# A hybrid attention and expert block: the first norm's factors applied behind the transposes of the first two tiles

## Chip, cores, metric

One core of a Trainium2 chip runs the whole block in one launch. The metric is the device time in microseconds. A profile names the engines PE (TensorE), DVE (VectorE), ACT (ScalarE), POOL (GpSimd) and SP (SyncE, which issues most DMAs).

## The reference

One layer on x of 1024 tokens by 1024 columns in float32, then a final norm:

```
hn   = rms_norm(h, norm_mix_g)
proj = hn @ w_in
y_dil, y_na = dilated_mixture_attention(...), neighbourhood_attention(...)
h = h + concat(rms_norm(y_dil), rms_norm(y_na)) @ w_out
h = h + hierarchical_moe(rms_norm(h, norm_ffn_g), ...)
return rms_norm(h, norm_final_g)
```

`rms_norm(x, gain)` scales each token (row) by `rsqrt(mean(x * x) + 1e-6)` and each column by its gain. The gain `norm_mix_g` holds 1024 factors, one per column of x. Here the change touches only how the first `rms_norm` reaches the product with `w_in`.

## The kernel before

Tokens are worked on in eight tiles of 128. The order of the work is written out by hand: the code's order is the order in each engine's queue, and a framework adds the semaphore waits. Matrix products keep float32 accuracy by splitting each operand into a high part and a rest (`split`, L102 to L104: ScalarE writes `hi` as a rounded copy, the subtraction of `hi` from the source gives `lo`, on VectorE or, with `pool=True`, on GpSimd); a product is three matmuls, hi·hi, hi·lo and lo·hi.

The stage that the change touches is the first one (L173 to L320). It norms x, transposes it so that the model's columns lie on the partitions (`xhi`, `xlo`, kept for all projections), and computes the values `v` of both attentions. Its parts:

- `x_stages(T)` (L192), a generator that is run step by step: Square with the row's sum on ScalarE, then mean and eps, Sqrt on ScalarE, the reciprocal, the scaling of x by the row's number and by `g_b` (L207, two halves of 512 columns). `g_b` holds the 1024 factors, repeated on all 128 partitions by one DMA (`bcast_row`, L126). After these four steps come two halves that each transpose four blocks of 128x128 into one PSUM bank (`ps_s`, `ps_pt`, L212) and split the bank into `xhi` and `xlo`.
- `wv_load` and `wv_split` (L182, L186) load and split a quarter of the value weights, two blocks of 128 rows each; `v_chunk(ps, T, w, c)` (L218) is the six matmuls of tile T with quarter c; `v_out` and `v_store` split and store the finished tile.
- Ahead of the data, TensorE runs 13 dummy matmuls on zeros (L242). ScalarE's first instruction is a Sqrt of a tile `one` (L255) that VectorE fills (L254), so that its table is loaded early.

SP issues in this order: x of tile 0, the identity, `g_b`, two quarters of the weights, x of tile 1, the other two quarters, x of tiles 2 and 3. TensorE's order is: dummies, tile 0's transposes, tile 0 with quarters 0 and 1, tile 1's transposes, tile 1 with quarters 0 and 1, tile 0 with quarters 2 and 3, tile 2's transposes, tile 1 with quarters 2 and 3, then tile by tile. The second projection of values, eight head pairs of attention, the output product and sixteen experts follow; the line L401 with L402 that the prediction speaks of is the split of a query bank in two pieces of 64 partitions each in the attention stage.

Of the kernel before, what the change touches and what calls it, by code (L numbers as in the profile page):

```python
# [9 lines left out]
F32 = mybir.dt.float32  # L10
F32R = mybir.dt.float32r
BF = mybir.dt.bfloat16
I32 = mybir.dt.int32
AF = mybir.ActivationFunctionType
ALU = mybir.AluOpType
# [57 lines left out]
def build(nc, tc, a, ctx, dbg=None):  # L73
    dbg = dbg or {}
    f = lambda t: t.bitcast(F32)
# [21 lines left out]
    ident = const.tile([128, 128], F32, name="ident")  # L97

    def bank(tag):
        return psum.tile([128, 512], F32, name="ps_" + tag, tag=tag)  # L100

    def split(hi, lo, src, pool=False):  # L102
        nc.scalar.activation(hi, src, AF.Copy)  # L103
        (nc.gpsimd if pool else nc.vector).tensor_tensor(lo, src, f(hi), op=ALU.subtract)  # L104
# [17 lines left out]
    def run(gen, n=1):  # L122
        for _ in range(n):
            next(gen, None)

    def bcast_row(dst, src, n):  # L126
        nc.sync.dma_start(dst, bass.AP(tensor=src.tensor, offset=src.offset, ap=[[0, 128], [1, n]]))
# [17 lines left out]
    with ExitStack() as att:  # L145
        xhi = [xt_pool.tile([128, 8, 512], F32R, name="xhi%d" % z, tag="xhi%d" % z) for z in range(2)]
        xlo = [xt_pool.tile([128, 8, 512], F32R, name="xlo%d" % z, tag="xlo%d" % z) for z in range(2)]
# [20 lines left out]
        def zero_low():  # L168
            for pair in k_low:
                for h, t in enumerate(pair):  # L170
                    nc.gpsimd.memset(f(t)[64 - 64 * h:128 - 64 * h, :], 0.0)

        with ExitStack() as ph:  # L173
            xp = ph.enter_context(tc.tile_pool(name="xp", bufs=2))
            wv = ph.enter_context(tc.tile_pool(name="wv", bufs=1))
            xs, raws = {}, {}
# [5 lines left out]
            def wv_load(c0, c):  # L182
                raws[c] = f(qk.tile([128, 1024], F32R, name="k_hh", bufs=4)).rearrange("p (k c) -> p k c", k=2)
                nc.sync.dma_start(raws[c], w_in.rearrange("(k p) c -> p k c", p=128)[:, 2 * c:2 * c + 2, c0:c0 + 512])

            def wv_split(c, pool=False):  # L186
                hi = wv.tile([128, 2, 512], F32R, name="wv_hi%d" % c)
                lo = wv.tile([128, 2, 512], F32R, name="wv_lo%d" % c)
                split(hi, lo, raws.pop(c), pool)
                return hi, lo  # L190

            def x_stages(T):  # L192

                xt = xs.pop(T)
                xn = xp.tile([128, 1024], F32, name="xn")
                ss = xp.tile([128, 1], F32, name="ss")
                nc.scalar.activation(xn, xt, AF.Square, accum_out=ss)
                yield
                nc.vector.tensor_scalar(ss, ss, 1.0 / 1024, EPS, op0=ALU.mult, op1=ALU.add)
                yield  # L200
                nc.scalar.activation(ss, ss, AF.Sqrt)
                yield
                r = xp.tile([128, 1], F32, name="rstd")
                nc.vector.reciprocal(r, ss)
                for q in range(2):
                    c = slice(512 * q, 512 * q + 512)
                    nc.vector.scalar_tensor_tensor(xn[:, c], xt[:, c], r, g_b[:, c], op0=ALU.mult, op1=ALU.mult)  # L207
                yield
                for q in range(2):
                    pt = bank("pt" if q else "s")  # L210
                    for k in range(4):
                        nc.tensor.transpose(pt[:, k * 128:(k + 1) * 128],  # L212
                                            xn[:, (4 * q + k) * 128:(4 * q + k + 1) * 128], ident)
                    s = slice(None), slice(4 * q, 4 * q + 4), slice(T % 4 * 128, (T % 4 + 1) * 128)
                    split(xhi[T // 4][s], xlo[T // 4][s], pt.rearrange("p (k t) -> p k t", k=4))
                    yield

            def v_chunk(ps, T, w, c):  # L218
                for k in range(2 * c, 2 * c + 2):
                    t = slice(T % 4 * 128, (T % 4 + 1) * 128)  # L220
                    for n, (x, l) in enumerate(((xhi, 0), (xhi, 1), (xlo, 0))):
                        nc.tensor.matmul(ps, x[T // 4][:, k, t], w[c][l][:, k % 2, :],
                                         start=k == 0 and n == 0, stop=k == 7 and n == 2)
# [15 lines left out]
            idle = xp.tile([128, 512], BF, name="idle", bufs=1)  # L239
            nc.gpsimd.memset(idle, 0.0)  # L240
            ps = bank("o")
            for _ in range(13):  # L242
                nc.tensor.matmul(ps, idle[:, 0:128], idle, start=True, stop=True)
            zero_low()
            nc.sync.dma_start(ident, a["ident"])
            g_b = wv.tile([128, 1024], F32, name="g_b")
            bcast_row(g_b, a["norm_mix_g"], 1024)
            wv_load(1024, 0)
            wv_load(1024, 1)
            x_load(1)  # L250
            for c in range(2, 4):
                wv_load(1024, c)
            one = xp.tile([128, 1], F32, name="one", bufs=1)
            nc.vector.memset(one, 1.0)  # L254
            nc.scalar.activation(one, one, AF.Sqrt)  # L255
            xt = {T: x_stages(T) for T in range(8)}
            run(xt[0], 4)
            w = {0: wv_split(0)}
            run(xt[0], 2)
            w[1] = wv_split(1)  # L260
            pv = [bank("mm"), bank("o")]
            v_chunk(pv[0], 0, w, 0)
            run(xt[1], 4)
            for c in range(2, 4):
                w[c] = wv_split(c, True)
# [17 lines left out]
            for T in range(2, 8):  # L283
                ps = bank("mm" if T % 2 else "o")
# [19 lines left out]
            for T in range(8):  # L304
                ps = bank("mm" if T % 2 else "o")
# [114 lines left out]
        ap = att.enter_context(tc.tile_pool(name="att", bufs=2))  # L420
# [279 lines left out]
        who, wlo, raws, yd, yt, hx = {}, {}, {}, {}, {}, {}  # L700
# [99 lines left out]
        for k in range(1, 8):  # L800
            s0 = 16 * (k - 1)
# [10 lines left out]
        for k in range(8):  # L812
            s = 104 + 2 * k if k < 4 else 106 + 2 * k
# [38 lines left out]
        ps, pts = {}, {}  # L852
        for s in range(len(steps) + 4):
            at = s % 16
            before = pairs[s // 16 - 1] if s >= 16 else None
            if s < len(steps):
                p, h, n = steps[s]
# [7 lines left out]
            if s - 2 in ps:  # L865
                q, g, m = steps[s - 2]
# [6 lines left out]
            if s - 3 in pts:  # L873
                q, g, m = steps[s - 3]
# [6 lines left out]
            if s + 6 < len(steps):  # L881
                if n == 2 and s > 8:
                    p.late_loads(h)
                after, g, _ = steps[8 * (s // 8) + 8] if s < 120 else (None, 0, 0)
# [264 lines left out]
    with ExitStack() as ph:  # L1149
# [113 lines left out]
        for T in range(8):  # L1263
            yn = y_norm(T)
            ns = norm_stages(T - 1) if T else None
            for c in range(2):
                ps = bank("mm")
# [93 lines left out]
    def new_x(name="xg"):  # L1361
        return ex.tile([128, 1024], F32, name=name, bufs=2)
# [367 lines left out]
    with tc.If(n_top > 256), tc.tile_pool(name="fb", bufs=1) as fb:  # L1730
# [10 lines left out]
        with tc.For_i(0, 16, 1) as e:  # L1741
# [9 lines left out]
            for q in range(6):  # L1751
                with tc.If(n_e > 256 + 128 * q):
                    x = new_x("xg1")
# [3 lines left out]
        for e in (14, 15):  # L1757
            W = whole(split_up([load_up(e, z) for z in range(2)], 0)) + split_down(load_down(e))
            n_e, = counts(ORDER[e], ORDER[e] + 1, mybir.ALL_ENGINES)
            for q in range(2):  # L1760
                with tc.If(n_e > 128 * q):
                    x = new_x("xg1")
# [32 lines left out]
```

## Time and profile before

| | |
|---|---|
| times of three runs | 888.94, 889.92, 892.41 us; median 889.92 |
| the profiled execution | 892.44 us, of which the span is 890.7 us |
| mean granted clock of TensorE over the span | 0.976 |
| busy: TensorE, VectorE, ScalarE, GpSimd | 832.3, 558.5, 510.0, 220.9 us |

The span is what the profiler sees of the engines; the device time has a little more around it. Times of single instructions below count from the start of the span. [...]

### The profile page before, as it was taken

What the parts mean: (1) busy time and instruction counts of PE and PEld (TensorE: products, weight loads), DVE (VectorE), ACT (ScalarE), POOL (GpSimd) and SP (SyncE); (2) the same over time, 40 slices, a digit from 0 to 9 for tenths busy, and PEclk for the clock granted to TensorE, in tenths of its full rate; (3) what the DMA queues carried; (4) which work ended last, traced back from release to release, by engine and by line L of the source; (5) the groups of instructions that cost most, each with busy time, mean ns of one, the idle gap of its engine ahead of it and who ended that gap; (6) DMA issues with size and microseconds to landing.
All of it is one profiled execution on the core that took longest, in us unless ns stands there. A gap on an engine that the chain in (4) does not pass through costs nothing. (4 is left out here: it accounts for less than half of the span.)

```text
span 890.7 us, 13312 instructions
## 1 busy us (share of the span) xinstructions
PE 832.3 (93%) x4492; PEld 693.2 (78%) x4492; DVE 558.5 (63%) x1249; ACT 510.0 (57%) x1079; POOL 220.9 (25%) x180
## 2 busy tenths in 40 slices
PE   8999999989999999999898999999799999999880
PEld 5888878979889888878787887887577787777760
DVE  4551125776767767666677753677786566959573
ACT  5441127757667576677575633543585566858570
POOL 4001122221232302332411100000442344635403
PEclk8999999999999999999999999998999999999995
DMA  6855452314343141534346747995798987999663
GB/s 238 286 210 165 126 159 65 105 48 108 96 136 105 54 137 48 148 100 120 76 160 195 265 144 239 357 343 216 233 354 250 317 220 209 357 324 304 181 257 121
DMA packets 129919, 168.72 MB, mean 189 GB/s; under 512 B 14875, under 2 KB 101403, under 8 KB 129824
## 3 DMA queue, kind: packets, MB, share of 16 engines
q1 hardware_dynamic: 119904, 143.58, 49.8%
q0 software_dynamic: 9936, 24.16, 9.8%
q8 instruction: 41, 0.67, 0.3%
q14 instruction: 38, 0.31, 0.1%
HBM read 129.93 MB, written 47.47 MB: 199 GB/s over the span
## 5 line engine op out<-in xcount | busy, mean ns | idle before, releaser
L103 ACT ACTIVATE pt_hi<-ps_pt 128x512 fp32r<-128x512 f32 (+2 forms) x128 | 67.6, 528 | 70.8 <-PE ps_pt L509 41.7
L378 PE MATMUL ps_mm<-xhi,w_lo 128*128 128x512 f32 x256 | 105.1, 411 | 1.1 <-POOL w_lo L104 1.1
L378 PE MATMUL ps_mm<-xlo,w_hi 128*128 128x512 f32 x256 | 105.0, 410 | 0.0
L378 PE MATMUL ps_mm<-xhi,w_hi 128*128 128x512 f32 x256 | 102.9, 402 | 0.0
L104 DVE TENSOR_TENSOR pt_lo<-ps_pt,pt_hi 128x512 fp32r<-128x512 f32 (+2 forms) x128 | 77.2, 603 | 31.8 <-ACT pt_hi L103 31.1
L104 POOL TENSOR_TENSOR w_lo<-w_raw,w_hi 128x1024 fp32r<-128x1024 f32 x16 | 38.3, 2392 | 229.5 <-ACT w_hi L103 229.5
L424 DVE CUSTOM_DVE_ANT_0 p<-ps_s,bias 128x256 f32<-128x256 f32 (+1 forms) x192 | 81.8, 450 | 18.2 <-PE ps_s L411 10.8
L104 DVE TENSOR_TENSOR g_lo<-raw_up,g_hi 128x1024 fp32r<-128x1024 f32 x64 | 75.5, 1220 | 25.2 <-ACT g_hi L103 25.1
L1419 PE MATMUL ps_mm<-g_hi,x_hi 128*128 128x512 f32 x184 | 76.0, 413 | 0.5 <-ACT x_hi L103 0.5
L1419 PE MATMUL ps_mm<-g_hi,x_lo 128*128 128x512 f32 x184 | 74.2, 403 | 2.2 <-DVE x_lo L104 2.2
L1419 PE MATMUL ps_mm<-g_lo,x_hi 128*128 128x512 f32 x184 | 73.9, 402 | 0.0
L430 ACT ACTIVATE p<-p,stats 128x256 f32<-128x256 f32 x128 | 63.7, 500 | 9.6 <-DVE stats L424 9.1
L103 ACT ACTIVATE g_hi<-raw_up 128x1024 fp32r<-128x1024 f32 x64 | 64.4, 1067 | 1.8 <-DMA raw_up<-in_w_up 0.8
L411 PE MATMUL ps_s<-k_hh,q_s 128*128 128x256 f32 (+1 forms) x192 | 60.7, 324 | 4.0 <-DMA k_hh<-k_hh 1.4
L411 PE MATMUL ps_s<-k_low,q_s 128*128 128x256 f32 (+1 forms) x192 | 62.6, 334 | 0.0
L411 PEld LDWEIGHTS ps_s<-k_hh,q_s 128*128 128x128 f32 x192 | 44.6, 232 | 10.9 <-DVE q_s L402 2.6
L378 PEld LDWEIGHTS ps_mm<-xhi,w_lo 128*128 128x128 f32 x256 | 48.7, 190 | 5.2 <-POOL w_lo L104 1.4
L1357 POOL DMA_INDIRECT xg<-hn_d,gi x30 | 41.3, 1377 | 40.1 <-PEq L1533 9.3
L378 PEld LDWEIGHTS ps_mm<-xhi,w_hi 128*128 128x128 f32 x256 | 48.7, 190 | 3.2
L378 PEld LDWEIGHTS ps_mm<-xlo,w_hi 128*128 128x128 f32 x256 | 48.4, 189 | 3.5
L411 PEld LDWEIGHTS ps_s<-k_low,q_s 128*128 128x128 f32 x192 | 44.6, 232 | 3.5
L430 ACT ACTIVATE p<-p,nm 128x384 f32<-128x384 f32 (+1 forms) x64 | 37.5, 586 | 15.2 <-DVE nm L424 14.8
(301 smaller groups left out, 2125.6 us busy)
## 6 DMA issues: line engine op xcount, KB each, us to landing
raw_up<-in_w_gate SPq DMA_DIRECT2D x32, 512.0 KB
raw_up<-in_w_up SPq DMA_DIRECT2D x32, 512.0 KB
raw_down<-in_w_down SPq DMA_DIRECT2D x16, 1024.0 KB
w_raw<-in_w_in SPq DMA_DIRECT2D x16, 512.0 KB
xt<-in_x SPq DMA_DIRECT2D x8, 512.0 KB
k_hh<-in_w_in SPq DMA_DIRECT2D x8, 512.0 KB
va_d<-vt SPq DMA_DIRECT2D x16, 256.0 KB
vb_d<-vt SPq DMA_DIRECT2D x8, 512.0 KB
```

The source lines that it names most:

```text
L103: nc.scalar.activation(hi, src, AF.Copy)
L104: (nc.gpsimd if pool else nc.vector).tensor_tensor(lo, src, f(hi), op=ALU.subtract)
L378: nc.tensor.matmul(ps, l[:, k, :], x[half][:, k, :], start=i == 0, stop=i == 23)
L411: nc.tensor.matmul(ps, self.q[h][:, qs], keys(k[h]), start=n == 0, stop=n == 1)
L424: nc.vector.tensor_tensor_reduce(out=p, in0=ps, in1=bias, scale=-0.125, scalar=3.0e38, op0=ALU.add, op1=ALU.min, accum_out=nm)
L430: nc.scalar.activation(p, p, AF.Exp, bias=nm, scale=-1.0, accum_out=l)
L1357: return nc.gpsimd.indirect_dma_start(out=x, out_offset=None, in_=src[:, :], in_offset=bass.IndirectOffsetOnAxis(ap=idx, axis=0), bounds_c ...
L1419: nc.tensor.matmul(ps, l[:, k, :], wt[:, k, :], start=i == 0, stop=i == 23)
```

## The change

For tiles 0 and 1 the scaling (L207) multiplies by the row's number alone. The column factors are applied when the transposed blocks leave PSUM: there a column of x is a partition, so a factor is one number per partition. `g_k` holds them, 128 partitions by 8 blocks. It is made of `g_row` (8 rows of 128, a DMA of 4 KB in `g_b`'s old place in SP's queue), transposed on TensorE into PSUM and copied by VectorE. Since each block has its own column of factors, a half tile is no longer split by two instructions on 512 columns but by four pairs on 128 columns. `g_b` itself is loaded behind the stage's four quarters of weights, for tiles 2 to 7.

The first quarter of the weights is split in two pieces, each ahead of a half of tile 0. The 13 dummy matmuls become 7 ahead of the transpose of `g_row`, 5 behind it, and 6 more behind tile 0's first six matmuls.

```diff
                 for q in range(2):
                     c = slice(512 * q, 512 * q + 512)
-                    nc.vector.scalar_tensor_tensor(xn[:, c], xt[:, c], r, g_b[:, c], op0=ALU.mult, op1=ALU.mult)
+                    if T < 2:
+                        nc.vector.tensor_scalar(xn[:, c], xt[:, c], r, None, op0=ALU.mult)
+                    else:
+                        nc.vector.scalar_tensor_tensor(xn[:, c], xt[:, c], r, g_b[:, c], op0=ALU.mult, op1=ALU.mult)
...
-                    split(xhi[T // 4][s], xlo[T // 4][s], pt.rearrange("p (k t) -> p k t", k=4))
+                    if T < 2:
+                        for k in range(4):
+                            hi, lo = [x[T // 4][:, 4 * q + k, t] for x in (xhi, xlo)]
+                            src, g = pt[:, k * 128:(k + 1) * 128], g_k[:, 4 * q + k:4 * q + k + 1]
+                            nc.scalar.activation(hi, src, AF.Copy, scale=g)
+                            nc.vector.scalar_tensor_tensor(lo, src, g, f(hi), op0=ALU.mult, op1=ALU.subtract)
+                    else:
+                        s = slice(None), slice(4 * q, 4 * q + 4), t
+                        split(xhi[T // 4][s], xlo[T // 4][s], pt.rearrange("p (k t) -> p k t", k=4))
...
-            for _ in range(13):
-                nc.tensor.matmul(ps, idle[:, 0:128], idle, start=True, stop=True)
+
+            def warm(n):
+                for _ in range(n):
+                    nc.tensor.matmul(ps, idle[:, 0:128], idle, start=True, stop=True)
+
+            warm(7)
             zero_low()
             nc.sync.dma_start(ident, a["ident"])
-            g_b = wv.tile([128, 1024], F32, name="g_b")
-            bcast_row(g_b, a["norm_mix_g"], 1024)
+            g_row = xp.tile([128, 128], F32, name="g_row", bufs=1)[0:8, :]
+            g_in = a["norm_mix_g"]
+            nc.sync.dma_start(g_row, bass.AP(tensor=g_in.tensor, offset=g_in.offset, ap=[[128, 8], [1, 128]]))
...
                 wv_load(1024, c)
+            g_b = wv.tile([128, 1024], F32, name="g_b")
+            bcast_row(g_b, a["norm_mix_g"], 1024)
+            g_k = xp.tile([128, 8], F32, name="g_k", bufs=1)
+            pt = bank("pt")
+            nc.tensor.transpose(pt[:, 0:8], g_row, ident[0:8, 0:8])
+            nc.vector.tensor_copy(g_k, pt[:, 0:8])
+            warm(5)
             one = xp.tile([128, 1], F32, name="one", bufs=1)
             nc.vector.memset(one, 1.0)
             nc.scalar.activation(one, one, AF.Sqrt)
             xt = {T: x_stages(T) for T in range(8)}
             run(xt[0], 4)
-            w = {0: wv_split(0)}
-            run(xt[0], 2)
+            w = {0: [wv.tile([128, 2, 512], F32R, name="wv_%s0" % n) for n in ("hi", "lo")]}
+            raw_v = raws.pop(0)
+            for k in range(2):
+                split(w[0][0][:, k], w[0][1][:, k], raw_v[:, k])
+                run(xt[0])
             w[1] = wv_split(1)
             pv = [bank("mm"), bank("o")]
             v_chunk(pv[0], 0, w, 0)
+            warm(6)
```

How this moves instructions shows in the queues. ScalarE's queue from its first instruction to tile 1's Square, before (the buffer numbers stand behind the names; `DVE`, `PE` and `DMAHW` in brackets are the engines or DMAs that an instruction waits for):

```order
L255 ACTIVATE one<-one 128x1 [waits DVE_49]
L197 ACTIVATE xn,ss<-xt 128x1024 [waits DMAHW0_49]
L201 ACTIVATE ss<-ss 128x1 [waits DVE_49]
L103 ACTIVATE wv_hi_150<-k_hh 128x1024 [waits DMAHW3_49]
L103 ACTIVATE xhi_82<-ps_s 128x4x128 [waits PE_49]
L103 ACTIVATE xhi_82<-ps_pt 128x4x128 [waits PE_49]
L103 ACTIVATE wv_hi_168<-k_hh 128x1024 [waits DMAHW4_49]
L197 ACTIVATE xn,ss<-xt 128x1024 [waits DMAHW5_49]
```

The same stretch with the change:

```order
L279 ACTIVATE one<-one 128x1 [waits DVE_49]
L197 ACTIVATE xn,ss<-xt 128x1024 [waits DMAHW0_49]
L201 ACTIVATE ss<-ss 128x1 [waits DVE_49]
L103 ACTIVATE wv_hi_155<-k_hh 128x512 [waits DMAHW3_49]
L223 ACTIVATE xhi_82<-ps_s,g_k 128x128 [waits PE_49]
L223 ACTIVATE xhi_82<-ps_s,g_k 128x128 [waits DVE_49] x3
L103 ACTIVATE wv_hi_155<-k_hh 128x512
L223 ACTIVATE xhi_82<-ps_pt,g_k 128x128 [waits PE_49]
L223 ACTIVATE xhi_82<-ps_pt,g_k 128x128 [waits DVE_49] x3
L103 ACTIVATE wv_hi_187<-k_hh 128x1024 [waits DMAHW4_49]
L197 ACTIVATE xn,ss<-xt 128x1024 [waits DMAHW5_49]
```

Two instructions on a bank of 512 columns became eight, and the second to fourth piece of each bank wait for VectorE, where the whole bank waited for TensorE alone. The second weights and tile 1's Square stand behind them.

VectorE's queue with the change, from its first instruction to the end of tile 0's split:

```order
L275 COPY g_k<-ps_pt 128x8 [waits PE_49]
L278 MEMSET one 128x1
L199 TENSOR_SCALAR ss<-ss 128x1 [waits Activation_49]
L204 RECIPROCAL rstd<-ss 128x1 [waits Activation_49]
L208 TENSOR_SCALAR xn<-xt,rstd 128x512 [waits DMAHW0_49,DVE_49]
L208 TENSOR_SCALAR xn<-xt,rstd 128x512
L104 TENSOR_TENSOR wv_lo_156<-k_hh,wv_hi_155 128x512 [waits DMAHW3_49,Activation_49]
L224 SCALAR_TENSOR_TENSOR xlo_84<-ps_s,g_k,xhi_82 128x128 [waits Activation_49] x4
L104 TENSOR_TENSOR wv_lo_156<-k_hh,wv_hi_155 128x512 [waits Activation_49]
L224 SCALAR_TENSOR_TENSOR xlo_84<-ps_pt,g_k,xhi_82 128x128 [waits Activation_49] x4
```

The memset of `one`, which was VectorE's first instruction, now stands behind the copy of `g_k`, which waits for TensorE's transpose of `g_row`; each piece of `xlo` waits for its piece of `xhi`.

## Rows read from the trace of the kernel before

**Rows 1.** Busy time by stretch: length, each engine (instructions), granted clock, DMA share, GB/s

```profile
0.00:8.00 8.00, 4.79 (x13) 1.63 (x13) 1.00 (x4) 2.84 (x5) 4.51 (x9) 1.00 0.68 222
8.00:15.25 7.25, 6.80 (x19) 4.74 (x20) 5.99 (x10) 5.91 (x9) 0.60 (x1) 0.53 1.03 401
15.25:40.00 24.75, 24.16 (x120) 19.39 (x119) 13.79 (x26) 10.72 (x24) 4.55 (x2) 1.00 0.64 217
```

**Rows 2.** Order of time, 0 to 9 us: start, duration, instruction [idle before, releaser]

```profile
0.82 0.06 DVE L254 MEMSET one<- 128x1 f32 x1 [0.82 <-PEq L1782]
1.33 4.79 PE L243 MATMUL ps_o<-idle 128*128 128x512 bf16 x13 [1.33 <-POOL idle L240]
...
2.04 0.20 ACT L255 ACTIVATE one<-one 128x1 f32<-128x1 f32 x1
...
4.34 1.06 ACT L197 ACTIVATE xn<-xt 128x1024 f32<-128x1024 f32 x1 [2.10 <-DMA xt<-in_x]
...
7.37 1.42 DVE L207 SCALAR_TENSOR_TENSOR xn<-xt,rstd,g_b 128x512 f32<-128x512 f32 x2 [1.26 <-DMA g_b<-in_norm_mix_g]
...
8.22 0.90 PE L212 MATMUL ps_s<-ident,xn 128*128 128x128 f32 x4 [2.11 <-issue]
8.60 1.06 ACT L103 ACTIVATE wv_hi<-k_hh 128x1024 fp32r<-128x1024 f32 x1 [2.69 <-DMA k_hh<-in_w_in]
```

**Rows 3.** DMA packets moved from 0 to 4.25 us, by size

```profile
DMA packets 317, 0.71 MB, mean 167 GB/s; under 512 B 32, under 2 KB 160, under 8 KB 317
```

**Rows 4.** Order of time, 11 to 28 us, columns as in rows 2

```profile
11.44 0.68 DVE L104 TENSOR_TENSOR xlo<-ps_pt,xhi 128x512 fp32r<-128x512 f32 x1
11.47 1.05 ACT L197 ACTIVATE xn<-xt 128x1024 f32<-128x1024 f32 x1
...
13.45 0.63 PE L222 MATMUL ps_mm<-wv_hi,xhi 128*128 128x512 f32 x1
...
13.46 1.99 ACT L103 ACTIVATE wv_hi<-k_hh 128x1024 fp32r<-128x1024 f32 x2
...
13.88 0.63 PE L222 MATMUL ps_mm<-wv_lo,xhi 128*128 128x512 f32 x1
...
17.29 1.07 ACT L197 ACTIVATE xn<-xt 128x1024 f32<-128x1024 f32 x1
...
17.55 0.68 DVE L104 TENSOR_TENSOR xlo<-ps_pt,xhi 128x512 fp32r<-128x512 f32 x1
...
19.10 1.92 DVE L207 SCALAR_TENSOR_TENSOR xn<-xt,rstd,g_b 128x512 f32<-128x512 f32 x2
...
20.09 0.39 PE L222 MATMUL ps_mm<-wv_hi,xhi 128*128 128x512 f32 x1
...
22.81 0.60 PE L212 MATMUL ps_s<-ident,xn 128*128 128x128 f32 x4
...
27.37 0.50 PE L222 MATMUL ps_o<-wv_hi,xlo 128*128 128x512 f32 x1 [0.33 <-DVE xlo L104]
```

**Rows 5.** Order of time, 131 to 133 us: a query bank split in two pieces

```profile
131.21 0.69 DVE L402 TENSOR_TENSOR q_s<-ps_mm,q_s 64x512 fp32r<-64x512 f32 x1 [3.56 <-ACT q_s L401]
131.93 0.59 ACT L401 ACTIVATE q_s<-ps_mm 64x512 fp32r<-64x512 f32 x1 [0.75 <-DVE q_s L402]
132.56 0.69 DVE L402 TENSOR_TENSOR q_s<-ps_mm,q_s 64x512 fp32r<-64x512 f32 x1 [0.66 <-ACT q_s L401]
```

**Rows 6.** Single operations by shape: busy us, mean ns | idle before

```profile
L103 ACT ACTIVATE a_hi<-ps_s 128x256 fp32r<-128x256 f32 x23 | 9.1, 397 | 3.6 <-PE ps_s L1428 3.6
...
L1423 DVE SCALAR_TENSOR_TENSOR act<-ps_mm,ws,sg 128x256 f32<-128x256 f32 x23 | 11.0, 480 | 33.1 <-ACT sg L1422 31.6 <-issue 1.5
...
L1112 DVE TENSOR_SCALAR d_hi<-iota,pk 128x256 bf16<-128x256 bf16 x16 | 3.9, 280 | 0.0
...
L1232 DVE SCALAR_TENSOR_TENSOR logits<-ps_pt,rsh,b_r 128x20 f32<-128x20 f32 x8 | 1.9, 235 | 0.8 <-PE ps_pt L1228 0.7
...
L571 DVE COPY sb<-ps_pt 128x32 f32<-128x32 f32 x4 | 0.8, 212 | 0.7 <-PE ps_pt L568 0.7
```

More of the change, by code (lines that the diff above doesn't have):

```diff
@@ L206, in x_stages @@
                     c = slice(512 * q, 512 * q + 512)
-                    nc.vector.scalar_tensor_tensor(xn[:, c], xt[:, c], r, g_b[:, c], op0=ALU.mult, op1=ALU.mult)
+                    if T < 2:
+                        nc.vector.tensor_scalar(xn[:, c], xt[:, c], r, None, op0=ALU.mult)
+                    else:
+                        nc.vector.scalar_tensor_tensor(xn[:, c], xt[:, c], r, g_b[:, c], op0=ALU.mult, op1=ALU.mult)
                 yield
+                t = slice(T % 4 * 128, (T % 4 + 1) * 128)
                 for q in range(2):
@@ L213, in x_stages @@
                                             xn[:, (4 * q + k) * 128:(4 * q + k + 1) * 128], ident)
-                    s = slice(None), slice(4 * q, 4 * q + 4), slice(T % 4 * 128, (T % 4 + 1) * 128)
-                    split(xhi[T // 4][s], xlo[T // 4][s], pt.rearrange("p (k t) -> p k t", k=4))
+                    if T < 2:
[7 more added lines that the diff above has]
+                        split(xhi[T // 4][s], xlo[T // 4][s], pt.rearrange("p (k t) -> p k t", k=4))
                     yield
```

## The prediction

> **What bounds the kernel now.** I read the busy times with the granted clock first, then the first 30 us in order of time, then single durations. The change touches only the first 30 us, and the view by stretches [rows 1] shows how they are spent. From 0 to 8 us TensorE runs only its 13 dummy matmuls (4.79 us). From 8 to 15.25 it is busy for 6.80 of 7.25 us, but at a granted clock of 0.53, mostly its lower level of 1.2 GHz. From 15.25 on it is busy for 24.16 of 24.75 us at 2.4 GHz. From there TensorE is the bound, so a microsecond by which its dense work starts later is a microsecond of the total. What matters is when tile 2's transposes can run (22.81 before, [rows 4]).
>
> The start [rows 2] is a chain. x arrives, the Square starts at 4.34, and reciprocal and scaling follow. The scaling starts at 7.37 after 1.26 us of idle time that the spread factors `g_b` ended, so it could have started at 6.11. The transposes start at 8.22. The first weights, queued behind `g_b`, release ScalarE at 8.60.
>
> Behind the chain lies slack. Tile 2's scaling takes 19.10 to 21.02 for both halves, so its first half is done near 20.06, but TensorE gets to the transposes at 22.81 [rows 4]: 2.75 us in which VectorE and ScalarE are ahead.
>
> **The change part by part.** The baseline is the profiled execution (span 890.7, time 892.44). The median of the three runs is 889.92, 2.5 below it; I add the sum to the median.
>
> *The wait for g_b goes, a detour comes.* The memset of `one` now stands behind the copy of `g_k` on VectorE, and ScalarE's first instruction, the table-warming root of `one`, waits for it; tile 0's Square is queued behind that root. So the Square waits for `ident` and `g_row` to land, a transpose, a copy, the memset and the root. When do they land? They stand behind x on one queue, so hardly before x's reader at 4.34. By 4.25 us 160 packets under 2 KB had moved, which holds all 128 rows of `ident` [rows 3]. The late end is 5.6, about as far again past 4.9; I take 4.9 as an estimate. Then a transpose of 0.29 at most (a 128x128 one at 2.4 GHz is part of a group of four in 0.60, [rows 4]), the copy 0.21 (128x32, [rows 6]), the memset under 0.1, the root 0.20 [rows 2] and hand-offs of about 0.04 each [rows 5]: the Square starts at 5.75, 1.4 later. From Square to the end of the reciprocal took 6.11 - 4.34 = 1.77, now until 7.5. The scaling starts 0.15 later than before: the gain of 1.26 is used up.
>
> *The scaling without g_b* is a TENSOR_SCALAR. The trace has none in float32 of 512 columns; 128x256 in bf16 takes 0.28 [rows 6], half of the STT is 0.71 (1.42 for two, [rows 2]). I take 0.56, twice the former, between these ends. First half ready at 8.1, transposes at 8.1 instead of 8.22, done by 9.0 if they take 0.90 as before.
>
> *The split of tiles 0 and 1 in quarters of a bank.* This is the large term. Before, a half tile was one ACTIVATE and one subtraction, and the next half overlapped. Now each half is four pairs, and the order shows that ScalarE's second to fourth piece each wait for VectorE. The trace of before has that pattern elsewhere: of the two pieces of one q bank [rows 5], ScalarE's second starts at 131.93, just when VectorE's first ends (131.21 + 0.69 = 131.90), although they use other partitions and other tiles. So a half is a chain A D A D A D A D. A, 128 columns from PSUM: 0.397 at 256 columns [rows 6] and 0.59 at 512 [rows 5] give 0.30 on their line. D, an STT from PSUM: 0.235 at 20 columns and 0.480 at 256 [rows 6] give 0.35. With two hand-offs (0.04 and 0.03) a pair is 0.72. Ends for a pair are the next rows on either side: 0.20 (one column, [rows 2]) + 0.235 + 0.07 = 0.51, and 0.397 + 0.480 + 0.07 = 0.95.
>
> [...]
>
> Now in order. Tile 0: first pair from 9.06, but VectorE has the first half of `wv_lo` to do until about 9.4; first half done at 11.9. ScalarE's second half of `wv_hi` (0.53, half of 1.06 in [rows 2]) runs behind the fourth A, VectorE's `wv_lo` follows until 12.65, then four D: done at 15.15. Before, the last xlo of tile 0 ended at 11.44 + 0.68 = 12.12 [rows 4]: 3.0 later. Behind it on ScalarE are queued the split of the second weights and tile 1's Square, 15.65 instead of 11.47. Scaling of tile 1 follows as before, first half at 18.2. ScalarE does two weight splits (1.99, [rows 4]) until 19.4, then tile 1's pairs: first half done at 19.4 + 4 x 0.72 = 22.3, second (its first A overlaps the last D) at 24.8, instead of 17.55 + 0.68 = 18.23 [rows 4]. Queued behind on ScalarE is tile 2's Square: 24.3 instead of 17.29, 7.0 later. Its scaling starts 1.81 later as before [rows 4], the first half is done at 26.8, and the transposes start at 26.85 instead of 22.81: 7.0 less the slack of 2.75, less 0.25 since the scaling of 1.92 there was stretched (1.42 otherwise). That is 4.0. TensorE's matmuls in between are no bound at 2.4 GHz: tile 1's first twelve follow the pairs until 22.5, and twelve more take 2.7 (20.09 to 22.81, [rows 4]), until 25.2. One stall goes: TensorE's 0.33 idle at 27.37 for tile 2's xlo [rows 4], about 0.5 with what its pipe loses, since ScalarE and VectorE now have more time there. **Sum: +3.5.**
>
> *Costs at nothing.* `g_b` behind the weights: needed at 25, long landed. The weights land about as much earlier as `g_b` took on the queue, but ScalarE now comes to them at 7.5, so at most a few tenths. The 5 more dummies and the transpose of `g_row` run while TensorE waits. SP's later loads and stores follow the work that frees their buffers.
>
> **The forecast** is 889.92 + 3.5 = 893.4. Ends: fifteen pairs on the path at 0.51 or 0.95 give -2.9 (TensorE then begins to cover) or +3.5; the landing of `g_row` -0.4 or +0.7; the scaling -0.5 or +0.3. Its own range is 890.5 to 896.5.
>
> **Rivals.** *A, the chain is hidden (faster).* If ScalarE's waits come too early to matter, a half costs VectorE's four D back to back, near 1.2 instead of 0.6, and tile 1's Square stays at about 11.7. Then the removed low-clock stretch counts: tile 0's second chunk and tile 1's transposes no longer run at half speed, tile 2's transposes come at 21.5, 1.3 earlier: 888.6. For it: the idle of [rows 2] and the low clock of [rows 1]. Against: [rows 5], the same wait in action. 0.10.
>
> *B, the clock stays low (slower).* TensorE idles between its dummies and its pieces until about 17. In the trace the clock fell during the idle time ahead of 8.22 and came back at 15.25 only, after 5 us of nearly dense work [rows 1, 2]. At the low level a matmul starts each 0.43 (13.45 to 13.88) instead of 0.23 [rows 4]. The 24 matmuls between tile 1's first pair and tile 2's transposes then take 24 x 0.43 = 10.3, until 29.8, and the transposes come 3.0 later still: 896.4. It decides once the low clock lasts beyond 23.5: n = (23.5 - 19.5) / 0.43 = 9 matmuls done by then, and 15 x 0.23 = 3.4 more end at 26.9. [...] 0.12. [...]
>
> *C, a later wait absorbs the delay*, so that nothing is left: 890.5. TensorE's density from 15.25 on [rows 1] speaks against it. 0.08.
>
> **How the numbers follow.** Forecast 0.70, A 0.10, B 0.12, C 0.08. The range 889.0 to 896.4 leaves out A and the outermost of the forecast and of B. About 0.5% (4.4 us) is what a measurement can tell from no change: slower begins at 894.4. A fifth of the forecast's case lies above that, with B 0.26; faster than 885.5 is 0.02; the rest, 0.72, is within.
>
> **What would show it.** ScalarE's pieces of `xhi` each start as VectorE's piece before ends, 0.72 apart; tile 0's Square starts near 5.75, tile 2's near 24; TensorE's transposes of tile 2 start near 26.9. If these start before 22.8, the forecast is wrong by rival A; if TensorE is at 1.2 GHz beyond 23.5, by B; a delay at 30 us that is gone at 105 us is C.

## The result, and the profile after

The changed kernel takes 896.93 us (median of four runs, 895.55 to 898.22); the kernel before 889.43 us (also four runs; three of them are those of the table above). The ratio is 1.0078, with a 95% interval of 1.0049 to 1.0108: slower by about 6.9 us. The forecast was 893.4, slower by 3.5, with a range up to 896.4: the measured time lies 0.5 above it. The sign and the mechanism were right, the size was half of what came. The profiled execution of the changed kernel took 897.64 us (span 895.8).

Busy time, granted clock and DMA by the same stretches as [rows 1], for the changed kernel:

```profile
0.00:8.00 8.00, 5.53 (x13) 1.65 (x14) 1.11 (x6) 3.25 (x6) 4.51 (x9) 1.00 0.76 246
8.00:15.25 7.25, 5.07 (x20) 2.43 (x20) 4.25 (x11) 3.71 (x10) 0.00 (x0) 0.91 0.99 386
15.25:40.00 24.75, 22.45 (x97) 17.02 (x96) 13.70 (x32) 13.89 (x30) 4.72 (x2) 0.89 0.42 137
```

TensorE lost 1.7 us of busy time between 8 and 15.25 and 1.7 more behind it, and in the last stretch its granted clock fell from 1.00 to 0.89. ScalarE is busier there by 3.2 us; tile 1's quarter pieces are in it.

In order of time, the first 10 us of the changed kernel (columns as in [rows 2]):

```profile
5.00 0.24 PE L274 MATMUL ps_pt<-ident,g_row 8*128 8x8 f32 x1 [0.50 <-DMA g_row<-in_norm_mix_g]
...
5.49 0.20 ACT L279 ACTIVATE one<-one 128x1 f32<-128x1 f32 x1 [3.45 <-DVE one L278]
...
5.59 1.04 ACT L197 ACTIVATE xn<-xt 128x1024 f32<-128x1024 f32 x1
...
7.38 0.88 DVE L208 TENSOR_SCALAR xn<-xt,rstd 128x512 f32<-128x512 f32 x2
...
8.02 0.63 PE L216 MATMUL ps_s<-ident,xn 128*128 128x128 f32 x4 [0.66 <-DVE xn L208]
...
8.69 0.37 ACT L223 ACTIVATE xhi<-ps_s,g_k 128x128 fp32r<-128x128 f32 x1 [1.02 <-PE ps_s L216]
...
9.09 0.35 DVE L224 SCALAR_TENSOR_TENSOR xlo<-ps_s,g_k,xhi 128x128 fp32r<-128x128 f32 x1 [0.22 <-ACT xhi L223]
...
9.47 0.37 ACT L223 ACTIVATE xhi<-ps_s,g_k 128x128 fp32r<-128x128 f32 x1 [0.42 <-DVE xlo L224]
...
9.88 0.35 DVE L224 SCALAR_TENSOR_TENSOR xlo<-ps_s,g_k,xhi 128x128 fp32r<-128x128 f32 x1 [0.44 <-ACT xhi L223]
```

The wait for `g_b` is gone, but the Square starts at 5.59 instead of 4.34, behind `one`, and the scaling starts at 7.38, where it started before (7.37, [rows 2]). Then comes the chain: each piece of `xhi` is released by the piece of `xlo` ahead of it, each piece of `xlo` by its `xhi`, and the pairs (one piece on each engine) follow each other by 0.79 us (8.69, 9.47, 10.26, 11.05). The list of waits from 0 to 45 us (us in total, times, longest) puts that pattern ahead of all other waits between these two engines:

```profile
DVE xlo L224 <- ACT xhi L223: 7.9, 14, 2.4
ACT xhi L223 <- DVE xlo L224: 5.4, 12, 0.8
```

In order of time, 14 to 29 us, where [rows 4] stood before:

```profile
14.93 0.35 DVE L224 SCALAR_TENSOR_TENSOR xlo<-ps_pt,g_k,xhi 128x128 fp32r<-128x128 f32 x1 [0.43 <-ACT xhi L223]
...
15.74 1.04 ACT L197 ACTIVATE xn<-xt 128x1024 f32<-128x1024 f32 x1
...
15.89 0.80 PE L234 MATMUL ps_mm<-wv_hi,xhi 128*128 128x512 f32 x1 [0.45 <-ACT wv_hi L103]
...
17.15 0.79 PE L234 MATMUL ps_mm<-wv_lo,xhi 128*128 128x512 f32 x1 [0.47 <-DVE ss L199]
...
18.59 0.63 PE L234 MATMUL ps_mm<-wv_lo,xhi 128*128 128x512 f32 x1
...
19.02 0.63 PE L234 MATMUL ps_mm<-wv_hi,xlo 128*128 128x512 f32 x1
...
19.45 1.06 PE L216 MATMUL ps_s<-ident,xn 128*128 128x128 f32 x4
...
20.54 0.37 ACT L223 ACTIVATE xhi<-ps_s,g_k 128x128 fp32r<-128x128 f32 x1 [1.25 <-PE ps_s L216]
...
25.79 1.05 ACT L197 ACTIVATE xn<-xt 128x1024 f32<-128x1024 f32 x1
...
28.48 0.63 PE L216 MATMUL ps_s<-ident,xn 128*128 128x128 f32 x4 [1.39 <-DVE xn L210]
```

Tile 0's split ends at 15.28 (14.93 + 0.35) instead of 12.12, tile 1's Square starts at 15.74 instead of 11.47, tile 2's at 25.79 instead of 17.29, and tile 2's transposes at 28.48 instead of 22.81: 5.67 later. TensorE, which waited for nothing there before, now waits 1.39 for the scaling. In front of tile 1's transposes stand the six matmuls of tile 0's second chunk. The second of them starts only at 17.15, when VectorE has written its `wv_lo` (15.87 to 17.10; the view names `ss`, the instruction behind it). From there they are 0.43 apart (18.59 to 19.02), the distance at the low clock; the granted clock was 0.50 in the stretches from 14 to 20 us:

```profile
14.00:16.00 2.00, 1.55 (x5) 0.37 (x3) 0.83 (x3) 1.58 (x4) 0.00 (x0) 0.50 0.51 209
16.00:18.00 2.00, 1.53 (x3) 0.93 (x4) 1.70 (x4) 1.68 (x4) 0.00 (x0) 0.50 0.00 0
18.00:20.00 2.00, 2.00 (x7) 1.51 (x7) 0.51 (x2) 1.29 (x2) 1.51 (x1) 0.50 0.21 29
```

Tile 3's transposes and the first matmul of the next stage, the projection of queries and keys, first before, then after:

```profile
31.13 0.60 PE L212 MATMUL ps_s<-ident,xn 128*128 128x128 f32 x4
...
108.00 0.39 PE L378 MATMUL ps_mm<-xhi,w_hi 128*128 128x512 f32 x1
```

```profile
36.55 0.60 PE L216 MATMUL ps_s<-ident,xn 128*128 128x128 f32 x4
...
115.12 0.40 PE L406 MATMUL ps_mm<-xhi,w_hi 128*128 128x512 f32 x1
```

Between the two TensorE ran without a wait of its own in both kernels. Tile 3 was 5.42 late, the projection 7.12: 1.70 more were lost where nothing waited. The stretch from 80 to 100 us shows how, first before, then after; the numbers in the first two brackets count TensorE's matmuls and its weight loads:

```profile
80.00:100.00 20.00, 20.00 (x90) 16.57 (x89) 2.77 (x4) 4.28 (x6) 3.46 (x2) 1.00 0.43 122
```

```profile
80.00:100.00 20.00, 20.00 (x88) 16.05 (x87) 2.77 (x4) 3.34 (x5) 2.40 (x1) 1.00 0.45 134
```

Both are full, at the full clock, and do the same matmuls, but 87 weight loads instead of 89 fit in. In the order of time the spacing, from the start of one matmul to the start of the next, is 0.2333 us after (28 matmuls from 30.02 to 36.32, 27 spacings) and 0.2267 before (the weight loads from 83.06 to 89.86, 30 spacings). The change doesn't touch these matmuls or their number. What it does touch is where the value weights lie, the operand of 512 columns (what TensorE loads as weights are the blocks of `xhi` and `xlo`): `g_row` (512 B per partition) and `g_k` (32 B) stand ahead of `wv_hi` and `wv_lo` in SBUF, and the built program places `wv_hi` at byte 121,312 of a partition before and at 121,856 after. Divided by 64 the first leaves 32, the second 0.

### The profile page after: what moved, and what is told of

Its sections match the earlier page's. It is cut to its first block, busy times and chain, and to the rows that moved or that the text cites. A ratio compares the mean times of both kernels' runs of the same rounds, so it can differ in the third digit from the quotient of the medians.

```text
span 895.8 us, 13352 instructions
## 1 busy us (share of the span) xinstructions
PE 835.3 (93%) x4498; PEld 691.8 (77%) x4498; DVE 560.2 (63%) x1263; ACT 513.8 (57%) x1092; POOL 211.3 (24%) x180
## 5 line engine op out<-in xcount | busy, mean ns | idle before, releaser
L1385 POOL DMA_INDIRECT xg<-hn_d,gi x30 | 36.7, 1225 | 37.2 <-PEq L1561 9.3
```

The costliest lines, as they stand in the source:

```text
L1385: return nc.gpsimd.indirect_dma_start(out=x, out_offset=None, in_=src[:, :], in_offset=bass.IndirectOffsetOnAxis(ap=idx, axis=0), bounds_c ...
```

## The experiments

My theory had three parts by then: the chain of quarter pieces sets most of the delay, the detour through `g_k` and TensorE's low clock add to it, and the place of the value weights sets the spacing. All ratios are to the kernel before, run on the same chip; positions in time are compared between single profiled executions.

### The place alone: `e1_shift`, `e2_unshift`, `e8_pad64`, `e9_pad96`

An unused tile is put ahead: in the kernel before (544 B behind `idle`), in the changed kernel (480 B), and in the kernel before ahead of the weight tiles alone (64 and 96 B).

```diff
             idle = xp.tile([128, 512], BF, name="idle", bufs=1)
+            xp.tile([128, 136], F32, name="pad", bufs=1)
```

```diff
             idle = xp.tile([128, 512], BF, name="idle", bufs=1)
+            xp.tile([128, 120], F32, name="pad", bufs=1)
```

```diff
             wv = ph.enter_context(tc.tile_pool(name="wv", bufs=1))
+            wv.tile([128, 16], F32, name="pad", bufs=1)
```

(24 instead of 16 columns in the last.) What was expected of the first two:

> The kernel before, with an unused tile of 544 B per partition in front of its other small tiles, so that the V-projection's weight tiles lie 544 B further, where the change has them; nothing of the work differs. Placement theory: the V stage's matmuls take the spacing that they have after the change (about 0.233 us, before 0.227), the first query-key projection matmul comes about 2 us later than before (110 instead of 108), and the time is about 891.5 us. Rival, that the placement does nothing and the wider spacing comes from what runs beside the matmuls: spacing 0.227, the first projection matmul at 108, the time of before (889.4) within 0.5.

> The changed kernel with an unused tile of 480 B per partition, which puts the V-projection's weight tiles on a place of the same remainder as before; nothing of the work differs. Placement theory: spacing back to 0.227 us, tile 2's transposes unmoved at 28.5, the first projection matmul about 2 us earlier than in the changed kernel (113 instead of 115.1), the time about 895. Rival, no effect of placement: spacing 0.233, the time of the changed kernel (896.9) within 0.5.

And of the other two, to see which remainder matters:

> The kernel before with an unused tile of 64 B per partition in front of the weight tiles of the V-projection alone: they move, but keep the remainder 32 when their place is divided by 64 (and lose that of 480 when divided by 512); the tiles of x and of the output stay. If the remainder by 64 matters: spacing 0.227 us, about 89 weight loads between 80 and 100 us, V stage ends at 108. If the remainder by 512 matters: 0.233, 87 loads, and the stage ends near 110.

> The kernel before with an unused tile of 96 B per partition in front of the weight tiles of the V-projection alone: remainder 0 by 64 and 64 by 512; the tiles of x and of the output stay. If the remainder by 64 matters: the slower spacing, about 87 weight loads between 80 and 100 us, and the first projection matmul some 86.5 to 87 us after tile 2's transposes. If it takes a remainder of 0 by 512: 89 loads and about 85.2 us.

The same stretch, 80 to 100 us, of the four kernels in this order:

```profile
80.00:100.00 20.00, 20.00 (x87) 16.10 (x86) 2.08 (x3) 2.75 (x4) 2.40 (x1) 1.00 0.44 125
```

```profile
80.00:100.00 20.00, 20.00 (x90) 16.57 (x89) 2.77 (x4) 3.34 (x5) 2.38 (x1) 1.00 0.45 128
```

```profile
80.00:100.00 20.00, 20.00 (x89) 16.39 (x89) 2.76 (x4) 4.29 (x6) 4.27 (x2) 1.00 0.41 118
```

```profile
80.00:100.00 20.00, 20.00 (x87) 16.12 (x86) 2.60 (x4) 3.90 (x6) 2.40 (x1) 1.00 0.43 126
```

The time from tile 3's transposes to the first projection matmul, a stretch in which TensorE waits for nothing, is a finer measure. It takes two values in all kernels run here but one, whatever else was changed (`e3_whole`, `e4_group`, `e5_one` and `e10_warm`, at the place of the changed kernel, have 78.57 or 78.58; `e7_all`, its repeat and `e11_tile0`, with the pad, 76.86 to 76.88):

| place of `wv_hi` | remainder by 64 | by 512 | kernels | tile 3 to projection, us |
|---|---|---|---|---|
| 121,312 | 32 | 480 | before | 108.00 - 31.13 = 76.87 |
| 122,336 | 32 | 480 | `e2_unshift` | 112.99 - 36.12 = 76.87 |
| 121,856 | 0 | 0 | after | 115.12 - 36.55 = 78.57 |
| 121,856 | 0 | 0 | `e1_shift` | 111.01 - 32.44 = 78.57 |
| 121,376 | 32 | 32 | `e8_pad64` | 107.30 - 29.96 = 77.34 |
| 121,408 | 0 | 64 | `e9_pad96` | 109.84 - 31.25 = 78.59 |

The place is shown as the cause: a pad alone makes the kernel before slower (893.23 us on 890.37, ratio 1.0026, 1.0015 to 1.0037), and a pad alone takes the 1.70 from the changed kernel (894.00, ratio 1.0037, 1.0024 to 1.0050, where the changed kernel had 1.0078; the two intervals only touch, so the trace carries this reading: the first projection matmul comes 2.13 earlier, 1.70 of it behind tile 3). The last two kernels move the weight tiles alone. The expected times of the first two were 891.5 and 895. For `e2_unshift` tile 2's transposes stayed at 28.20. The remainder by 64 carries most of it: with 0 the stretch takes 78.57 to 78.59, also where the remainder by 512 is 64. But `e8_pad64` lies between (77.34, 0.47 above the fast value), which neither theory had; whatever makes this part stays open, and so does why the place matters at all. The times of the last two, 890.42 and 893.28, are one execution each and settle nothing.

Three of these kernels differ from the kernel before by an unused tile alone, and yet their start varies. The scaling waits for `g_b` for 1.26 us in the kernel before [rows 2], and with a pad for 2.11 (`e1_shift`), 0.60 (`e8_pad64`) and 0.46 (`e9_pad96`), and tile 2's transposes come at 22.81, 24.05, 21.62 and 22.85. So of the 3.01 us by which `e1_shift` is late at the projection 1.31 stand already at tile 3 and are not the spacing's, and a difference of a microsecond from the 22.81 or the 108.00 of the kernel before is within this spread.

### The split taken whole: `e3_whole`

```diff
-                        for k in range(4):
-                            hi, lo = [x[T // 4][:, 4 * q + k, t] for x in (xhi, xlo)]
...
+                        s = slice(None), slice(4 * q, 4 * q + 4), t
+                        split(xhi[T // 4][s], xlo[T // 4][s], pt.rearrange("p (k t) -> p k t", k=4))
```

> The changed kernel with the first two tiles' split taken whole-bank as before the change; it leaves out the multiplication by the norm's factors for these two tiles. Chain theory (the quarter pieces that hand over between ScalarE and VectorE set the delay): tile 0's split ends near 11.5 instead of 14.93, tile 2's transposes come at 22.5 to 23.5 instead of 28.48, and the time falls by 4 to 6 us, to about 892. Rival, that TensorE's low granted clock sets the delay whatever the split costs: tile 2's transposes stay later than 26 and the time falls by less than 2. Rival, that the later start is absorbed: transposes near 23 and a time within 1 us of the changed kernel.

In order of time, tile 0's first half's split and tile 2's transposes:

```profile
8.66 0.60 ACT L103 ACTIVATE xhi<-ps_s 128x512 fp32r<-128x512 f32 x1 [1.01 <-PE ps_s L216]
...
9.29 0.69 DVE L104 TENSOR_TENSOR xlo<-ps_s,xhi 128x512 fp32r<-128x512 f32 x1 [0.45 <-ACT xhi L103]
...
21.18 0.60 PE L216 MATMUL ps_s<-ident,xn 128*128 128x128 f32 x4
```

Two instructions, 1.32 us from start to end, stand where the chain of eight takes 3.11 (8.69 to 11.80). Tile 2's transposes come 7.30 earlier than in the changed kernel (earlier than the expected 22.5), and the clock is 1.00 in every stretch from 8 to 24 us. The time is 891.21, ratio 1.0001 (0.9987 to 1.0014). So the split in pieces makes the whole delay of tile 2, the low clock included, which did not come in this execution. Pieces and hand-offs went together here; the next run takes them apart. The transposes are also 1.63 earlier than in the kernel before, but 0.44 against `e8_pad64`: what the change would gain without its price is not shown. The place of the weights costs its 1.70 in this kernel too (78.57): the first projection matmul is at 108.13.

### The pieces grouped by engine: `e4_group`

```diff
+                        parts = []
                         for k in range(4):
                             hi, lo = [x[T // 4][:, 4 * q + k, t] for x in (xhi, xlo)]
...
+                            parts.append((hi, lo, pt[:, k * 128:(k + 1) * 128], g_k[:, 4 * q + k:4 * q + k + 1]))
+                            nc.scalar.activation(hi, parts[k][2], AF.Copy, scale=parts[k][3])
+                        for hi, lo, src, g in parts:
                             nc.vector.scalar_tensor_tensor(lo, src, g, f(hi), op0=ALU.mult, op1=ALU.subtract)
```

> The changed kernel with the same sixteen pieces per tile in another order: four on ScalarE, then four on VectorE, of each half. Chain theory (the handoff between the engines for every piece is the cost, not the pieces' number): ScalarE's pieces run back to back and VectorE's follow one behind, so a half takes about 1.9 us (four times 0.37 and one 0.35) or, with the two engines on one bank at once, some 1.3 to 1.9, instead of 3.15; tile 2's transposes come at 23.5 to 25 and the time falls by 3.5 to 5 us, to 892 to 893.5. Rival, that the two engines can not read one bank at the same time, whatever the order: the half still takes 2.9 to 3.2 us and the time stays within 1 us of 896.9.

Tile 0's first half, tile 1's first half and tile 2's transposes, in order of time:

```profile
9.02 1.13 ACT L224 ACTIVATE xhi<-ps_s,g_k 128x128 fp32r<-128x128 f32 x4
...
10.18 1.12 DVE L226 SCALAR_TENSOR_TENSOR xlo<-ps_s,g_k,xhi 128x128 fp32r<-128x128 f32 x4 [0.34 <-ACT xhi L224]
...
17.52 1.14 ACT L224 ACTIVATE xhi<-ps_s,g_k 128x128 fp32r<-128x128 f32 x4 [1.25 <-PE ps_s L216]
...
18.69 1.13 DVE L226 SCALAR_TENSOR_TENSOR xlo<-ps_s,g_k,xhi 128x128 fp32r<-128x128 f32 x4 [3.21 <-ACT xhi L224]
...
24.33 0.60 PE L216 MATMUL ps_s<-ident,xn 128*128 128x128 f32 x4
```

Both theories were half right. VectorE's first piece starts only when ScalarE's fourth is done (10.15 and 10.18, 18.66 and 18.69): the built program has it wait for the fourth, so the two engines do take turns on one bank. Whether they could read it at the same time, no run here shows. But four pieces in a row take 1.13: each takes 0.34 to 0.38, and they start 0.25 (ScalarE) and 0.26 (VectorE) apart. A half takes 2.28 instead of 3.11. The next half's `xhi` runs beside this half's `xlo`. Tile 2's transposes come 4.15 earlier, the first projection matmul 3.82 (111.30), and the time is 891.37, ratio 1.0005 (0.9994 to 1.0015): 5.6 us less by the medians for the same instructions in another order.

The order is not the whole price. Grouped, the pieces still bring tile 2's transposes 3.15 later than the whole-bank split (24.33 against 21.18), and the granted clock is low here too (0.51 from 14 to 16 us). Of the 7.30 that the split in pieces cost, 4.15 came from the order and 3.15 stayed, 0.36 of it since the first half starts later in this execution (9.02 against 8.66).

### The detour: `e5_one`

```diff
+            one = xp.tile([128, 1], F32, name="one", bufs=1)
+            nc.vector.memset(one, 1.0)
+            nc.scalar.activation(one, one, AF.Sqrt)
             g_k = xp.tile([128, 8], F32, name="g_k", bufs=1)
```

(and the three lines are taken out behind the copy of `g_k`.)

> The changed kernel with the unit factor's memset and the square root that follows it put ahead of the copy of the turned factors on VectorE, so that ScalarE no longer waits for the turned factors. Detour theory (the path from the factors' landing through TensorE, VectorE and ScalarE delays tile 0's sum of squares by what the sum called 1.4 us, and the delay runs on to the end): ScalarE's first Square starts at 4.3 to 4.5 instead of 5.59, tile 0's transposes at 6.8 to 7.2 instead of 8.02, tile 2's at 27.2 to 27.6 instead of 28.48, and the time is about 895.8 (1.0 to 1.3 below the changed kernel). Rival, that the weights of the first chunk decide (its first split waits for their transfer): Square earlier, but tile 2's transposes stay within 0.4 us of 28.48, and the time within 0.5 of 896.9.

In order of time, tile 0's Square and transposes and tile 2's transposes:

```profile
4.39 1.06 ACT L197 ACTIVATE xn<-xt 128x1024 f32<-128x1024 f32 x1 [2.14 <-DMA xt<-in_x]
...
6.82 0.63 PE L216 MATMUL ps_s<-ident,xn 128*128 128x128 f32 x4 [0.47 <-DVE xn L208]
...
26.18 0.63 PE L216 MATMUL ps_s<-ident,xn 128*128 128x128 f32 x4 [1.40 <-DVE xn L210]
```

The Square and tile 0's transposes come 1.2 earlier, as the detour theory had it. Tile 2's come 2.30 earlier, more than expected: the granted clock is 1.00 from 16 to 20 us, where it was 0.50 (here it was 0.50 from 11 to 14), so with the earlier start TensorE also had its clock back in time. The time is 895.42 (expected 895.8), ratio 1.0054 (1.0042 to 1.0066).

### The clock: `e10_warm`

```diff
                         nc.tensor.matmul(ps, x[T // 4][:, k, t], w[c][l][:, k % 2, :],
                                          start=k == 0 and n == 0, stop=k == 7 and n == 2)
+                    if cold:
+                        warm(cold.pop())
```

(with `cold.append(8)` ahead of tile 0's first chunk.)

> The changed kernel with eight further idle matmuls behind the first three matmuls of tile 0's first chunk, to fill TensorE's idle time between 9.9 and 12.0. Clock theory (the low granted clock between 14 and 21 delayed tile 1's transposes by about 1.2 us): the clock stays at 1.00 to 20, the second chunk's last matmul starts near 18.0 instead of 19.02, tile 1's transposes at 18.4 to 18.7 instead of 19.45, and tile 2's 0.8 to 0.9 earlier, at about 27.6. Rival, that the splits of the weights set these times whatever the clock: tile 1's transposes within 0.3 us of 19.45 and tile 2's within 0.3 of 28.48.

Busy times by stretch (columns as in [rows 1]), and in order of time the transposes of tiles 1 and 2:

```profile
12.00:16.00 4.00, 2.64 (x10) 1.09 (x10) 2.10 (x6) 2.40 (x6) 0.00 (x0) 1.00 0.76 295
16.00:20.00 4.00, 3.10 (x16) 2.18 (x17) 2.51 (x6) 3.26 (x7) 1.56 (x1) 1.00 0.04 7
```

```profile
18.37 0.60 PE L216 MATMUL ps_s<-ident,xn 128*128 128x128 f32 x4
...
27.07 0.63 PE L216 MATMUL ps_s<-ident,xn 128*128 128x128 f32 x4 [1.40 <-DVE xn L210]
```

The clock stays at 1.00 and tile 1's transposes come 1.08 earlier, tile 2's 1.41: the low clock cost that much, a little more than the 0.8 to 0.9 expected. The first projection matmul is 1.41 earlier too (113.71). The one time taken, 898.29, doesn't show it; the four runs of the changed kernel lie 2.7 apart, and the last expert matmul starts at 871.7 here, later than in the changed kernel (871.2), though both run the same code behind the projection. A difference of this size drowns in the later stages' spread.

### All three edits, and tile 1 taken back: `e7_all`, `e7_again`, `e11_tile0`

`e7_all` joins `e4_group`, `e5_one` and the 480 B of `e2_unshift`. `e11_tile0` adds to it:

```diff
-                    if T < 2:
+                    if T < 1:
```

(in both places.)

> The changed kernel with three edits together: the pieces grouped by engine, the unit factor's path taken off the turned factors, and the unused tile of 480 B. If the three parts add (pieces 5.5, detour 1.2, placement 2.5): the matmul spacing is 0.227, tile 2's transposes come at about 23, and the time is 887.5 to 888.5 on a kernel before of 890.4, a ratio of about 0.997. Rival, that some of it is absorbed once the weights' transfers bound the start: transposes of tile 2 at 24 or later and a ratio of 0.999 to 1.000.

> The three edits together once more, beside the kernel that takes tile 1 back: the ratio to the kernel before between 0.997 and 0.9995, as first measured (0.9984), if that gain holds; a ratio of 1.000 or more if it was the spread of the runs.

> The kernel with the three edits together, and tile 1 done as tiles 2 and later (spread factors in its scaling, whole-bank split), so that only tile 0 takes the factors behind its transposition. If the spread factors have landed by 13.9, when tile 1's scaling starts: the first half's scaling takes 0.75 instead of 0.44 and no more waits come; tile 1's split ends near 17.5 instead of 18.8, TensorE's waits between 16.2 and 17.1 (0.4) shrink, and tile 2's transposes come 0.3 to 0.6 earlier than 22.16; the time is 0.3 to 0.6 below that of the three edits (889.0 on 890.7). Rival, the factors land later than that: tile 1's scaling waits for a transfer, and the time is the same or above.

`e7_all` takes 889.01 us (12 runs) on 890.66, ratio 0.9984 (0.9971 to 0.9996); again, 888.94 (12 runs) on 890.55, ratio 0.9989 (0.9975 to 1.0004). It is the fastest kernel here, 1.0 to 1.4 us ahead of the kernel before, though the second interval just includes no difference; the expected 887.5 to 888.5 was missed by half a microsecond. Tile 2's transposes are at 22.16, the stretch from tile 3 to the projection takes 76.88, and the first projection matmul comes at 107.37, 7.75 earlier than in the changed kernel, where the three edits alone gave 3.82, 2.29 and 2.13. So the parts very nearly add, up to the next stage. That this is 0.63 ahead of the kernel before is within the spread of that kernel's start.

Taking tile 1 back lost it again in the trace: tile 2's transposes come at 23.89 instead of 22.16, the first projection matmul at 109.08 instead of 107.37. The time is 890.69 on 890.55, ratio 1.0007 (0.9986 to 1.0028), an interval that overlaps those of `e7_all`. In order of time:

```profile
14.32 3.54 DVE L210 SCALAR_TENSOR_TENSOR xn<-xt,rstd,g_b 128x512 f32<-128x512 f32 x2 [0.60 <-DMA g_b<-in_norm_mix_g]
...
14.61 5.50 POOL L104 TENSOR_TENSOR wv_lo<-k_hh,wv_hi 128x1024 fp32r<-128x1024 f32 x2 [9.36 <-ACT wv_hi L103]
...
23.89 0.60 PE L216 MATMUL ps_s<-ident,xn 128*128 128x128 f32 x4
```

The rival held: the scaling waits 0.60 for `g_b`. Then its two halves take 3.54 instead of 1.42 [rows 2]: the first 0.75, the second 2.87 (14.98 to 17.85), beside the first of GpSimd's two subtractions (14.61 to 17.30).

## Why the prediction was right, and where it was short

The direction and the path of the delay came as forecast, at twice the size, and 0.5 us beyond the range. The range's upper end was also set below what its own terms gave: the pair at 0.95 alone makes +3.5, that is 896.9, before the ends of the landing and the scaling are added.

- *The detour eats the gain of the removed wait:* right. The Square was forecast for 5.75 and came at 5.59; the scaling came 0.01 later than before, forecast 0.15. `g_row` released its transpose at 5.00; the landing estimate was 4.9. `e5_one` shows the price, 1.2 us for tile 0.
- *Scaling without `g_b`:* 0.44 for a half (0.88 for two), forecast 0.56.
- *The chain A D A D:* right as a mechanism, shown by the releasers and by `e4_group`. The pair was sized at 0.72 and took 0.786: D was 0.35 as forecast, A 0.37 where the line through two longer rows [rows 5, 6] gave 0.30. The rest is two hand-offs of 0.03 (9.06 to 9.09, 9.44 to 9.47). Four pieces in a row on one engine, in `e4_group`, start only 0.25 (ScalarE) and 0.26 (VectorE) apart; in the chain each piece costs its whole duration.
- *Tile 0's end and tile 1's Square:* forecast 15.15 and 15.65, measured 15.28 and 15.74. This nearness is in part luck: the first pair began at 8.69, 0.37 before the forecast's 9.06, and the longer pairs used that up.
- *Tile 1's pairs from 19.4:* **this step failed.** I let them start when ScalarE was free (it was, at 19.29). They started at 20.54, because tile 1's transposes stood behind the six matmuls of tile 0's second chunk in TensorE's queue, and these ran 0.43 apart at the low clock. I had called TensorE's matmuls in between no bound at the full clock, and priced the low clock only for the matmuls behind tile 1's first pair (rival B). But it was low from 14 to 20, in front of the transposes. It put the first pair 1.14 later; longer pairs added 0.35 up to tile 2's Square, and 0.14 more came up to its transposes: 28.48 instead of 26.85. `e10_warm`, with the clock at 1.00, has the first pair at 19.15 and tile 2's transposes 1.41 earlier: that is the clock's part. No run shows a frequency: the 2.4 and 1.2 GHz of the prediction, its sum included, stand for the granted clock of 1.00 and 0.50, at which matmuls on 512 columns start 0.227 to 0.233 us and 0.43 us apart.
- *One stall goes:* it went, but from tile 2's to tile 3's transposes only 0.25 was gained (8.07 instead of 8.32), where I had taken 0.5: 0.33 of idle time [rows 4] and an estimate for what the pipe loses, which no run shows by itself. The wider spacing takes about 0.2 of it (30 spacings); at the old place of the weights, in `e2_unshift`, it was 0.40 (7.92).
- **A term was missing:** the same matmuls, 0.233 apart instead of 0.227, 1.70 up to the next stage. The list of costs at nothing did not name the new tiles' place in SBUF at all; nothing in the trace of before could price it, but the shift of 544 B could be seen in the built program.

Together: forecast 4.04 - 0.5 = 3.54; plus 1.63, 0.25 and 1.70 makes 7.12, the delay of the first projection matmul in this pair of traces. That the ratio's 6.9 us lies so near is partly luck: the start of the kernel before and of its padded copies varies by over 2 us, and at the end these two executions are only 5.1 apart (spans of 895.8 and 890.7).

Rival A (the chain is hidden) fell with the releasers. Rival B's condition, a low clock beyond 23.5, did not come about, but its cause did, earlier in the queue: the clock fell after TensorE's waits (1.92 ahead of 11.99 and 0.22 ahead of 12.71; the granted clock is 0.93 from 13.5 to 14 and 0.50 from there), as `e10_warm` shows by its reverse. It was back at 1.00 from 21 on (0.74 from 20.5 to 21). In the trace of before, too, the clock was 1.00 until 8.25 and fell just behind the idle time (2.11 ahead of 8.22; 0.94 from 8 to 8.5, then 0.50), not during it as I had read. Rival C (a later wait absorbs it) fell: the delay of 5.42 at tile 3 was never made up in this stage. What came, slower by 0.78%, had been given 0.26; the 0.72 for "within 0.5%" was too much as pair, clock and placement all came out on the same side.

## What to carry to other kernels

When a split is cut in pieces that two engines read from one PSUM bank, count hand-offs as well as instructions: alternating, a pair cost 0.79 us; with four on one engine and then four on the other, the same sixteen instructions for a tile brought tile 2 forward by 4.15 us (5.6 us of 896.9 in time). Some 3 us of the delay stayed with the pieces. When an engine is to wait in a prologue, look at what stands behind it on TensorE at the clock that it may have after the wait (here 0.50, with matmuls 0.43 apart instead of 0.23), not only at who waits for the data. And when a small tile is added, compare the spacing of matmuls far from the edit and see in the built program which tiles have moved: a pad of 480 B was worth 1.70 us here.

## What the runs showed that I had not expected

- The spacing of matmuls on 512 columns depends on where the operand of 512 columns lies: 0.227 us at two places with remainder 32 by 64 and 0.233 at two with remainder 0, at the same granted clock of 1.00 and with no wait; at a third place with remainder 32 it lay between (`e8_pad64`, 0.229: 30 spacings in 6.87 us).
- The scaling by `g_b` (`SCALAR_TENSOR_TENSOR`, 128x512 in float32, both operands in SBUF) takes 0.75 alone. In six traces one starts while a subtraction of GpSimd's weight split is running, and each ends 0.55 or 0.56 us behind that subtraction: in `e11_tile0` it takes 2.87 (to 17.85, GpSimd's to 17.30), in `e8_pad64` 2.12 (20.09 and 19.54), in the kernel before 1.25 (20.35 and 19.80). So it looks like a wait and not like slower work. The other way round, GpSimd's subtraction takes 2.69 to 2.84 where such a scaling is running when it starts, and 2.36 to 2.40 where none is.
- Eight more dummy matmuls in an idle stretch of two microseconds (`e10_warm`) kept the clock at 1.00 and brought tile 2's transposes 1.41 us forward, though the dummies do no work.
